# Loads of small vectors kept in program order, and two cache copies cut into sixteen in a later phase

## The chip, the cores and the metric

The kernel runs on one core of one Trainium2 chip. The metric is the device time of one execution in microseconds (us). TensorE (PE) multiplies, with its own weight-load sequencer (PEld); VectorE is DVE, ScalarE is ACT, GpSimd is POOL. SyncE (SP) computes nothing here: it issues every DMA of the kernel, one after the other.

## What is computed

One inference step of a one-layer decoder, all in float32, for a prompt group of 2048 rows and a sample group of 8 x 8 rows. The reference cut to what matters:

```
h = rms_norm(x, norm_w)
q, k, v, z_a, z_s, xbc, dt_raw, g = split(h @ w_in)
o_a = sliding-window attention(rope(norm(q)), rope(norm(k)), v, sinks)
xbc = silu(causal_conv(xbc, conv_w) + conv_b)
dt  = softplus(dt_raw + dt_bias);  A = -exp(A_log)
y   = chunked scan(x, dt, A, B, C) + D_skip * x
o_s = group_norm(y * silu(z_s)) * ssd_norm_w
out = x + (sigmoid(g_a) * (o_a * silu(z_a)) @ w_attn + sigmoid(g_s) * o_s @ w_ssd) @ w_out
k_win_sample = concat(cache_k, k_new)[:, -128:]        (the same for v)
```

The last line concerns the change: of each of the 8 samples, 120 of the 128 old rows of both caches go unchanged into an output, from DRAM to DRAM (8 x 120 x 1 KB = 960 KB for each cache).

## The kernel before

The work is in three phases. **T1** (`phase_t1`) takes the prompt in four blocks of 512 rows (b = 0 to 3): it normalizes and transposes the rows (`prep_first`, `prep_h`), stores the result to the scratch `h_d`, projects q, k, v and the attention's gate z_a, and does the attention. It begins with block 0; `prep_h` of the next block is done beside a block. **S** (`phase_s`) loads the same rows again (`load_h`), projects x, B, C, z_s and dt, and does the scan, in four blocks of four groups g (16 steps); at the end of each step `stats` sends a row of sums through DRAM (`ss_d` -> `sr` -> `rs_d`). **T2** does the samples (`phase_sa`, `phase_ss`) and the output projections.

Every float32 product is made of three matmuls: a weight tile lands in `raw` (L157, two buffers), ACT casts it into the high half of `whl` (L150), DVE makes the low half (L151), and PE multiplies (z_a: L171; q, k, v, dt: L195; phase S: L184). One load of `raw` is 1 MB, two of half that for z_a.

The program is written in one order and put into another by a scheduler, which simulates the engines and hoists work to where it thinks that it fits; an instruction under `keep_in_program_order` isn't hoisted. Each engine then runs its own list strictly in order, SP too. On SP each DMA takes the next of eight semaphores, so a DMA can't be issued before the one eight places ahead of it has completed.

The places that the change and the prediction speak of:

- `init3` (L227 to L246) loads what only phases S and T2 use: three strips of rows (conv weights, bias, norm weight), which PE transposes (L233, L234); `sinkS` in 16 loads of 8 x 1 elements (L238), which DVE negates (L239); `A_bc` (L240), which ACT exponentiates (L241) and DVE negates (L242); `dtb_bc` (L243); and `Dcol` in two loads (L246), each of 64 partitions x 16 elements of 4 bytes, taken with a stride of two from D_skip. It is called at the start of block 3 (L586), but the scheduler has put 20 of its 23 loads among those of block 0.
- L643 copies the caches; it is written in `phase_sa`, after phase S, and the scheduler has put it at the kernel's start as well.
- In T1 the first z_a tiles of block 0 end in ACT's tanh (`th`, L420) and DVE's `zs` (L421). `norm_x` of block 1 begins with ACT's square (`junk`, L251), which reads `xt`, loaded at L290. On ACT's list the first of these squares stands ahead of the third tanh.

Of the kernel before, what the change touches and what calls it, by code (L numbers as in the profile page):

```python
# [17 lines left out]
P = 128  # L18
# [60 lines left out]
def build(tc, nc, a, o, seq, phases=("T1", "S", "T2"), dbg=None):  # L79
    NB = seq // TB  # L80
    V, A, G, PE, SY = nc.vector, nc.scalar, nc.gpsimd, nc.tensor, nc.sync
# [9 lines left out]
    def ct_(name, shape, dtype=F32):  # L91
        return const.tile(shape, dtype, name=name, tag=name)
# [44 lines left out]
    sinkS = ct_("sinkS", [P, 1])  # L137
    nsinkS = ct_("nsinkS", [P, 1])
    A_bc = ct_("A_bc", [P, 32])
    dtb_bc = ct_("dtb_bc", [P, 32])  # L140
    Dcol = ct_("Dcol", [P, 16])
# [69 lines left out]
    def rpow(dst, src, scale, eps, tmp):  # L211
        G.tensor_scalar(tmp, src, scale, eps, ALU.mult, ALU.add)
        G.tensor_tensor(dst, tmp, mhalf[: dst.shape[0], : dst.shape[1]], ALU.pow)


    def init2():
# [7 lines left out]
            SY.dma_start(wrow[:, i, 72:80], w[0:8].partition_broadcast(P))  # L224
        V.tensor_scalar(wrow[:, 0], wrow[:, 0], 0.125, None, ALU.mult)

    def init3(xp, trp):  # L227
        rows = xp.tile([P, 2, P], F32, name="rows3", tag="xt")
        SY.dma_start(rows[:96, 0], a["conv_w"][0].rearrange("k (c p) -> (k c) p", p=P))
        SY.dma_start(rows[96:120, 0], a["conv_b"][0].rearrange("(c p) -> c p", p=P))  # L230
        SY.dma_start(rows[:16, 1], a["ssd_norm_w"][0].rearrange("(c p) -> c p", p=P))
        ips = trp.tile([P, 256], F32, name="tr", tag="tr")
        PE.transpose(ips[:, :120], rows[:120, 0], ident[:120, :120])  # L233
        PE.transpose(ips[:, 128:144], rows[:16, 1], ident[:16, :16])  # L234
        V.tensor_scalar(cwb.rearrange("p k c -> p (k c)"), ips[:, :120], 0.5, None, ALU.mult)
        V.tensor_copy(snw, ips[:, 128:144])
        for h in range(NH):
            SY.dma_start(sinkS[8 * h : 8 * h + 8], a["sinks"][0][h : h + 1].partition_broadcast(8))  # L238
        V.tensor_scalar(nsinkS, sinkS, -1.0, None, ALU.mult)  # L239
        SY.dma_start(A_bc, a["A_log"][0].partition_broadcast(P))  # L240
        A.activation(A_bc, A_bc, AF.Exp)  # L241
        V.tensor_scalar(A_bc, A_bc, -1.0, None, ALU.mult)  # L242
        SY.dma_start(dtb_bc, a["dt_bias"][0].partition_broadcast(P))  # L243
        dv = a["D_skip"][0].rearrange("(c l) -> l c", l=2)
        for hl in range(2):
            SY.dma_start(Dcol[64 * hl : 64 * hl + 64], dv[hl].partition_broadcast(64))  # L246

    def norm_x(xt, jp, nwb, n=P):
        st = jp.tile([P, 3], F32, name="rs", tag="rs", bufs=2)[:n]
# [61 lines left out]
    def load_h(b, smp):  # L311
        hT = []
        for k in range(KT):
            ht = cur["h"].tile([P, 2, cur["hw"]], F32R, name="hT", tag="hT")
            SY.dma_start(ht[:, :, :TB].bitcast(F32), h_d[b][k // 4][:, k % 4])
            if smp:
                split(ht[:, 0, TB:], ht[:, 1, TB:], hs[:, k])
            hT.append(ht)
        return hT
# [56 lines left out]
    def phase_t1():  # L376
        with ExitStack() as es:
# [205 lines left out]
            for b in range(NB):  # L583
                hT = nxt
                if b == NB - 1:
                    init3(xp, trp)  # L586
                for pair in range(2):
                    zs = zap.tile([P, HG, TB], F32, name="zs", tag="zs")
                    if pair == 0:
                        for hgp in range(2):  # L590
                            za_tile(b, pair, hgp, hT, zs)
                        tab = tables(b)
                        k_tile(b, hT, tab)
                        v_tile(b, hT)
                    qTs = [q_tile(b, 2 * pair + kvl, hT, tab) for kvl in range(2)]
                    if pair == 0 and b + 1 < NB:
                        prep_h(b + 1, xp, jp, trp, nwb)
                        if b + 1 == sb:
                            prep_s(xp, jp, trp, nwb)
                    if pair == 1:  # L600
                        for hgp in range(2):
                            za_tile(b, pair, hgp, hT, zs)
                    if pair == 1 and b + 1 < NB:
                        nxt = load_h(b + 1, False)
                    for tt in range(NT):
                        attn_unit(b, pair, tt, [qTs[0][tt], qTs[1][tt]], zs)

    def phase_sa(oas):
        with ExitStack() as es:
# [18 lines left out]
            for jj in range(2):  # L628
# [3 lines left out]
                for i in range(4):  # L632
                    j, hl = (4 * jj + i) // 2, (4 * jj + i) % 2
# [6 lines left out]
                SY.dma_start(kn_d[:, half * P : half * P + P], kr[64 * half : 64 * half + 64, :2].rearrange("p h d -> p (h d)"))  # L640
            for nm, scr in (("k", kn_d), ("v", vn_d)):
                ow = o[f"{nm}_win_s"]
                SY.dma_start(ow[:, 0:120], a[f"cache_{nm}"][0].rearrange("b j h d -> b j (h d)")[:, 8:P])  # L643
                SY.dma_start(ow[:, 120:P], scr.rearrange("(b t) c -> b t c", b=8))
            KN = one.tile([64, NKV, 64], F32, name="KN")
            tr = trp.tile([64, 2, P], F32, name="tr", tag="tr")
# [7 lines left out]
            for b in range(8):  # L654
# [30 lines left out]
                for pair in range(2):  # L685
                    for kvl in range(2):
                        kv = 2 * pair + kvl
                        dst = po[64 * kvl : 64 * kvl + 64, pair, b]
# [29 lines left out]
    def phase_s():  # L718
        with ExitStack() as es:
# [50 lines left out]
            def dt_block(b):  # L770
                sh = [NT, 32]
                dt = dp.tile([P] + sh, F32, name="dt", tag="dt")
                SY.dma_start(dt, dt_d[b])
                softplus(dt, dt, dtb_bc.unsqueeze(1).to_broadcast([P] + sh), P, sh, dp, "sp")
                dA = dp.tile([P] + sh, F32, name="dA", tag="dA", bufs=1)
                V.tensor_tensor(dA, dt, A_bc.unsqueeze(1).to_broadcast([P] + sh), ALU.mult)
                dA2 = dA.rearrange("p c h -> p (c h)")
                ps = trp.tile([P, 3, P], F32, name="tr", tag="tr")
                PE.matmul(ps[:, 0], tri, dA2, start=True, stop=True)
                PE.matmul(ps[:, 1], ones, dA2, start=True, stop=True)  # L780
                PE.matmul(ps[:, 2], dA2, tri, start=True, stop=True)
                acs = dp.tile([P, P], F32, name="acs", tag="acs")
                V.tensor_copy(acs, ps[:, 0])
                at = dp.tile([P, P], F32, name="at", tag="at", bufs=1)
                V.tensor_copy(at, ps[:, 2])
                SY.dma_start(ac_d[b], at)
                dec = dp.tile([P, P], F32, name="dec", tag="dec")
                A.activation(dec, ps[:, 1], AF.Exp)
                wd = dp.tile([P, P], F32, name="wd", tag="wd")
                V.tensor_tensor(wd, ps[:, 1], acs, ALU.subtract)  # L790
                A.activation(wd, wd, AF.Exp)
                V.tensor_tensor(wd, wd, dt.rearrange("p c h -> p (c h)"), ALU.mult)
                return dt.rearrange("p c h -> p (c h)"), acs, dec, wd
# [118 lines left out]
            def stats(b, g):  # L912
                r = dp.tile([P, 4], F32, name="sr", tag="sr")
                SY.dma_start(r, ss_d[b][g].rearrange("o (p c) -> p (o c)", c=4))
                r2 = dp.tile([P, 4], F32, name="sr2", tag="sr2")
                rpow(r, r, 1.0 / 512, 4 * EPS, r2)
                SY.dma_start(rs_d[b][g].rearrange("(p c) -> p c", c=4), r)

            for b in range(NB):
                dts_ = dt_block(b)  # L920
                hT = load_h(b, b == sb)
                for g in range(4):
                    ssd_group(b, g, *proj_group(b, g, hT), *dts_)
                    stats(b, g)
            cur["hT"] = hT
            for g in range(4):
                tr = trp.tile([P, 4, P], F32, name="tr", tag="tr")
# [358 lines left out]
    if "S" in phases:  # L1286
        phase_s()
# [41 lines left out]
```

## Time and profile before

| | |
|---|---|
| median of 3 runs | 3202.14 us (3200.97 to 3202.41) |
| the profiled execution's own time | 3201.39 us |
| its span | 3199.6 us |
| PE / DVE / ACT / POOL busy | 96% / 65% / 44% / 31% |
| mean granted TensorE clock | 0.989 of full speed |

The profile comes from one execution. The span is the time from the first to the last instruction that the profiler saw; 1.8 us of the execution lie outside it. Times in the views are counted from the span's start. Block 3 of T1 begins at about 620 us, phase S at about 717, T2 at about 2000.

### The profile page before, as it was taken

How to read it: one execution, taken by the hardware profiler on the slowest of the kernel's cores; microseconds unless marked ns; L12 is line 12 of the kernel's file. 1: busy time of each engine (PE TensorE's matmuls, PEld its weight loads, DVE VectorE, ACT ScalarE, POOL GpSimd, SP SyncE). 2: the span in 40 equal slices, each digit the busy share in tenths (PEclk: the TensorE clock that was granted, in tenths of full speed). 3: DMA queues.
4: the chain of work that ended last, by engine and by line, in shares of the span. 5: the costliest groups of instructions: out<-in, count | busy, mean ns of one | idle time of the engine just before them, and what ended most of it. 6: DMA issues, size and time to landing. Idle time of an engine off the chain costs nothing.

```text
span 3199.6 us, 49248 instructions
## 1 busy us (share of the span) xinstructions
PE 3085.4 (96%) x19038; PEld 2649.2 (83%) x19038; DVE 2081.5 (65%) x3265; ACT 1419.9 (44%) x2786; POOL 982.5 (31%) x905
## 2 busy tenths in 40 slices
PE   6999999998999999999999998999999999999999
PEld 5978787877899877777777776787877799999888
DVE  3877868787777787888878886455555554334433
ACT  3544535455555555555656564333233333222321
POOL 1523232231445555555656664000121100000000
PEclk8999999999999999999999998999999999999999
DMA  6544425333433544444454444445655564345443
GB/s 215 157 141 117 141 76 180 108 107 103 126 121 119 172 130 124 154 148 131 129 167 147 129 141 128 139 131 154 205 181 143 155 206 132 99 132 175 137 107 103
DMA packets 472931, 448.88 MB, mean 140 GB/s; under 512 B 33824, under 2 KB 420664, under 8 KB 472648
## 3 DMA queue, kind: packets, MB, share of 16 engines
q1 hardware_dynamic: 472696, 445.73, 45.2%
q8 instruction: 150, 2.46, 0.3%
q14 instruction: 85, 0.70, 0.1%
HBM read 382.39 MB, written 65.35 MB: 140 GB/s over the span
## 4 chain that ended last, share of the span: by engine, by line
PE 73%; DVE 12%; DMA 5%; POOL 5%; issue 3%; ACT 2%; SPq 0%; POOLq 0%; DVEq 0%; ACTq 0%
PE mm L184 46%; PE mm L195 12%; PE mm L171 5%; DVE acc L760 3%; DVE whl L151 2%; POOL L L857 2%; DMA raw<-in_w_in_dram 2%; PE sc L522 1%; PE tr L551 1%; POOL ws L881 1%; DVE zs L897 1%; PE tr L539 1%; PE st L884 1%; DMA xt<-in_x_prompt_dram 1%; ACT whl L150 1%
## 5 line engine op out<-in xcount | busy, mean ns | idle before, releaser
L184 PE MATMUL mm<-hT,whl 128*128 128x512 f32 (+1 forms) x6720 | 1349.1, 357 | 10.4 <-DMA hT<-h_d 4.1
L184 PEld LDWEIGHTS mm<-hT,whl 128*128 128x128 f32 x6720 | 1119.5, 190 | 181.1 <-issue 12.6
L151 DVE TENSOR_TENSOR whl<-raw,whl 128x2048 fp32r<-128x2048 f32 (+1 forms) x232 | 524.6, 2265 | 280.4 <-ACT whl L150 273.0
L184 PE MATMUL mm<-ot,whl 128*128 128x512 f32 (+1 forms) x2880 | 569.1, 355 | 2.8 <-DVE whl L151 2.5
L184 PEld LDWEIGHTS mm<-ot,whl 128*128 128x128 f32 x2880 | 474.2, 188 | 74.9 <-issue 5.7
L150 ACT CAST whl<-raw 128x2048 fp32r<-128x2048 f32 (+1 forms) x232 | 412.7, 1786 | 263.3 <-PE mm L184 132.5
L195 PE MATMUL mm<-whl,hT 128*128 128x256 f32 (+1 forms) x2304 | 307.8, 289 | 23.7 <-DVE zs L421 17.2
L195 PEld LDWEIGHTS mm<-whl,hT 128*128 128x128 f32 x2304 | 290.7, 192 | 28.2 <-DVE zs L421 17.9
L760 DVE SCALAR_TENSOR_TENSOR acc<-cr,cwb,acc 128x512 f32<-128x512 f32 x288 | 284.5, 990 | 15.8 <-ACT acc L755 7.0
L857 POOL TENSOR_TENSOR L<-L,cbm 128x1024 f32<-128x1024 f32 x64 | 182.5, 2861 | 94.4 <-DVE cbm L846 92.8
L195 PE MATMUL mm<-whl,ot 128*128 128x256 f32 (+1 forms) x1632 | 203.9, 285 | 0.0
L195 PEld LDWEIGHTS mm<-whl,ot 128*128 128x128 f32 (+1 forms) x1632 | 197.6, 188 | 5.3 <-issue 4.9
L171 PE MATMUL mm<-hT,whl 128*128 128x512 f32 x768 | 194.3, 403 | 2.3 <-ACT hT L277 2.1
L855 ACT ACTIVATE L<-AB,acs 128x128 f32<-128x128 f32 x512 | 157.0, 389 | 38.6 <-PE py L878 29.0
L171 PEld LDWEIGHTS mm<-hT,whl 128*128 128x128 f32 x768 | 142.8, 192 | 33.8 <-ACT hT L277 2.5
L368 ACT ACTIVATE s<-s,ng 128x128 f32<-128x128 f32 x256 | 99.9, 393 | 94.4 <-DVE ng L362 84.2
L150 ACT CAST ot<-v 128x512 fp32r<-128x512 f32 x96 | 58.9, 620 | 162.1 <-DVE v L1195 86.9
L881 POOL TENSOR_TENSOR ws<-wx,ws 128x512 fp32r<-128x512 f32 x64 | 112.2, 1752 | 10.1 <-ACT ws L880 9.8
L374 POOL TENSOR_SCALAR s<-s,den 128x128 f32<-128x128 f32 x128 | 50.1, 403 | 202.7 <-DVE den L370 140.6
L826 ACT ACTIVATE th<-mm 128x512 f32<-128x512 f32 (+1 forms) x80 | 40.0, 509 | 160.8 <-PE mm L184 153.6
L764 ACT ACTIVATE th<-acc 128x512 f32<-128x512 f32 x96 | 60.5, 630 | 111.8 <-DVE acc L760 111.7
L1187 ACT ACTIVATE t<-mm 128x512 f32<-128x512 f32 (+1 forms) x76 | 37.6, 518 | 162.4 <-PE mm L184 141.9
(318 smaller groups left out, 3912.5 us busy)
## 6 DMA issues: line engine op xcount, KB each, us to landing
raw<-in_w_in_dram SPq DMA_DIRECT2D x120, 1024.0 KB
hT<-h_d SPq DMA_DIRECT2D x80, 512.0 KB
raw<-in_w_in_dram SPq DMA_DIRECT2D x64, 512.0 KB
AB<-ac_d SPq DMA_DIRECT2D x64, 512.0 KB
raw<-in_w_ssd_proj_dram SPq DMA_DIRECT2D x32, 1024.0 KB
v_d<-zs SPq DMA_DIRECT2D x16, 1024.0 KB
v<-v_d SPq DMA_DIRECT2D x64, 256.0 KB
raw<-in_w_attn_proj_dram SPq DMA_DIRECT2D x64, 256.0 KB
```

Source lines behind the costliest of these rows:

```text
L150: A.copy(hi, src)
L151: V.tensor_tensor(lo, src, hi.bitcast(F32), ALU.subtract)
L171: PE.matmul(ps, hl[:, x, k, c0 : c0 + P], ht[:, y, :], start=first and i == 0, stop=last and i == n - 1,)
L184: PE.matmul(ps, hl[:, x, k, c0 : c0 + P], ht[:, y, lo : lo + n], start=i == 0, stop=i == 3 * len(hT) - 1,)
L195: PE.matmul(ps, ht[:, x, tt * P : tt * P + m], hl[:, y, k, :n], start=i == 0, stop=i == 3 * len(hT) - 1,)
L368: A.activation(s[:, i, :width], s[:, i, :width], AF.Exp, bias=ng[:, i : i + 1], accum_out=den[:, i : i + 1])
L374: G.tensor_scalar(s[:, i, :width], s[:, i, :width], den[:, i : i + 1], 0.5, ALU.mult, ALU.mult)
L760: V.scalar_tensor_tensor(out=acc, in0=raw[:, k : k + TB], scalar=cwb[:, k, ct : ct + 1], in1=acc, op0=ALU.mult, op1=ALU.add)
L764: A.activation(th, acc, AF.Tanh)
L855: A.activation(L[:, h], AB[:, h], AF.Relu, scale=-1.0, bias=acs[:, hc.start + h : hc.start + h + 1])
L857: G.tensor_tensor(L, L, cbm[:, c].unsqueeze(1).to_broadcast([P, 8, P]), ALU.mult)
L881: G.tensor_tensor(ws[:, 1], wx, ws[:, 0].bitcast(F32), ALU.subtract)
```

## The change

A helper `late` issues a DMA that is kept in program order. All 23 loads of `init3` go through it. The two cache copies leave `phase_sa`; in their place phase S copies one sample's rows of k and one sample's of v (120 KB each, 16 x 1920 elements) behind `stats` of groups 1 and 3 of each block, 16 DMAs in all, through `late` as well.

```diff
+    def late(dst, src):
+        tc.keep_in_program_order(SY.dma_start(dst, src))
+
     def init3(xp, trp):
         rows = xp.tile([P, 2, P], F32, name="rows3", tag="xt")
-        SY.dma_start(rows[:96, 0], a["conv_w"][0].rearrange("k (c p) -> (k c) p", p=P))
+        late(rows[:96, 0], a["conv_w"][0].rearrange("k (c p) -> (k c) p", p=P))
...
         for h in range(NH):
-            SY.dma_start(sinkS[8 * h : 8 * h + 8], a["sinks"][0][h : h + 1].partition_broadcast(8))
+            late(sinkS[8 * h : 8 * h + 8], a["sinks"][0][h : h + 1].partition_broadcast(8))
         V.tensor_scalar(nsinkS, sinkS, -1.0, None, ALU.mult)
-        SY.dma_start(A_bc, a["A_log"][0].partition_broadcast(P))
+        late(A_bc, a["A_log"][0].partition_broadcast(P))
...
-            SY.dma_start(Dcol[64 * hl : 64 * hl + 64], dv[hl].partition_broadcast(64))
+            late(Dcol[64 * hl : 64 * hl + 64], dv[hl].partition_broadcast(64))
...
                 ow = o[f"{nm}_win_s"]
-                SY.dma_start(ow[:, 0:120], a[f"cache_{nm}"][0].rearrange("b j h d -> b j (h d)")[:, 8:P])
                 SY.dma_start(ow[:, 120:P], scr.rearrange("(b t) c -> b t c", b=8))
...
                     stats(b, g)
+                    for nm in ("k", "v"):
+                        for r in range((4 * b + g) * 8 // (4 * NB), (4 * b + g + 1) * 8 // (4 * NB)):
+                            late(o[f"{nm}_win_s"][r, 0:120], a[f"cache_{nm}"][0, r, 8:P].rearrange("j h d -> j (h d)"))
```

What this does to the engines' lists stands below at three places. With the change, line numbers are three higher from L227 on, two higher behind L643 (L157 and the others ahead of `init3` stay); the loads and copies that go through `late` bear its line, L228.

**The start, SP.** Before, from the last of the small loads on (`xt` is block 1's input, `h_d` a store of the normalized rows, `raw` a weight tile):

```order
L240 DMA A_bc<-in_A_log_dram 128x32
L282 DMA h_d_1_61<-hT 128x1024
L243 DMA dtb_bc<-in_dt_bias_dram 128x32
L246 DMA Dcol<-in_D_skip_dram 64x16x1 x2
L290 DMA xt<-in_x_prompt_dram 128x1024
L282 DMA h_d_1_61<-hT 128x1024
L290 DMA xt<-in_x_prompt_dram 128x1024
L643 DMA out_dram<-in_cache_k_dram 8x2x15360
L282 DMA h_d_1_61<-hT 128x1024
L643 DMA out_dram<-in_cache_v_dram 8x2x15360
L157 DMA raw<-in_w_in_dram 128x8x256 x3
```

The same stretch of SP's list with the change:

```order
L577 DMA tab_2442<-in_rope_p_dram 128x4x80
L285 DMA h_d_1_61<-hT 128x1024 x2
L293 DMA xt<-in_x_prompt_dram 128x1024 x2
L285 DMA h_d_1_61<-hT 128x1024 x2
L157 DMA raw<-in_w_in_dram 128x8x256 x3
L476 DMA dt_d_112<-dtt 128x128
```

The 20 small loads and both copies are gone from this stretch; both loads of `xt` stand behind two stores of `h_d` and nothing of `init3`. ACT's list loses the exponential of A_bc, DVE's the negations of sinkS and A_bc; the rest keeps its order.

**T1's last block, SP and PE.** SP before, at the start of block 3 (`oa_d` is a store of block 2's attention, `dt_d` of its dt; the six `raw` of 128x8x128 are the next z_a tiles):

```order
L157 DMA raw<-in_w_in_dram 128x8x256
L563 DMA oa_d_1_73<-zs 128x4x128
L473 DMA dt_d_115<-dtt 128x128
L157 DMA raw<-in_w_in_dram 128x8x128 x6
L157 DMA raw<-in_w_in_dram 128x8x256
```

With the change:

```order
L157 DMA raw<-in_w_in_dram 128x8x256
L566 DMA oa_d_1_73<-zs 128x4x128
L228 DMA rows_6540<-in_conv_w_dram 96x128
L228 DMA rows_6540<-in_conv_b_dram 24x128
L228 DMA rows_6540<-in_ssd_norm_w_dram 16x128
L228 DMA sinkS<-in_sinks_dram 8x1 x16
L228 DMA A_bc<-in_A_log_dram 128x32
L228 DMA dtb_bc<-in_dt_bias_dram 128x32
L228 DMA Dcol<-in_D_skip_dram 64x16x1 x2
L476 DMA dt_d_115<-dtt 128x128
L157 DMA raw<-in_w_in_dram 128x8x128 x6
```

All 23 loads now stand ahead of the six z_a loads. PE's list there before, around the transposes of the strips (`tr<-PT,vT` is an attention output, `tr<-cst,kd` transposes k):

```order
L551 MATMUL tr<-PT,vT 64x512 x4
L233 MATMUL tr<-cst,rows_6540 128x120
L234 MATMUL tr<-cst,rows_6540 128x16
L453 MATMUL tr<-cst,kd 128x128 x4
L195 MATMUL mm<-whl,hT 128x256 x38
```

PE's list at the same place with the change:

```order
L554 MATMUL tr<-PT,vT 64x512 x4
L195 MATMUL mm<-whl,hT 128x256 x80
L236 MATMUL tr<-cst,rows_6540 128x120
L237 MATMUL tr<-cst,rows_6540 128x16
L456 MATMUL tr<-cst,kd 128x128 x4
L195 MATMUL mm<-whl,hT 128x256 x38
```

80 matmuls have come ahead of the two transposes. On DVE's list the copies out of the transposes, the negation of sinkS and that of A_bc stand a little behind them, on ACT's the exponential of A_bc behind the cast of the next weight tile.

**The end of T1, PE.** Before, from the last products of T1 (L171) to the first of phase S (L184); `tr<-cst,s` and `tr<-PT,vT` belong to the attention, `tr<-cst,qr` transposes the last q:

```order
L171 MATMUL mm<-hT,whl 128x512 x12
L539 MATMUL tr<-cst,s 128x128 x4
L551 MATMUL tr<-PT,vT 64x512 x4
L496 MATMUL tr<-cst,qr 128x128 x12
L184 MATMUL mm<-hT,whl 128x288 x20
L522 MATMUL sc<-KTT,qT 128x256 x4
```

With the change:

```order
L171 MATMUL mm<-hT,whl 128x512 x6
L542 MATMUL tr<-cst,s 128x128 x8
L554 MATMUL tr<-PT,vT 64x512 x4
L499 MATMUL tr<-cst,qr 128x128 x8
L525 MATMUL sc<-KTT,qT 128x256 x4
L499 MATMUL tr<-cst,qr 128x128 x4
L184 MATMUL mm<-hT,whl 128x288 x23
```

One attention unit more stands between the last products of T1 and the first of phase S. In phase S itself the lists of PE, DVE, ACT and POOL keep their order; SP's gets the copies, each pair right behind the store `rs_d` of its step.

## Rows read from the trace of the kernel before

**Rows 1.** The page: busy us (share of the span) xinstructions.

```profile
PE 3085.4 (96%) x19038; PEld 2649.2 (83%) x19038; DVE 2081.5 (65%) x3265; ACT 1419.9 (44%) x2786; POOL 982.5 (31%) x905
```

**Rows 2.** Waits, 40 to 84 us: total us, times, longest.

```profile
DVE zs L421 <- ACT th L420: 22.0, 2, 21.3
ACT junk L251 <- DMA xt<-in_x_prompt_dram: 21.9, 2, 20.9
PE mm L195 <- DVE zs L421: 17.2, 2, 16.1
...
DVE nsinkS L239 <- DMA h_d<-hT: 5.1, 1, 5.1
ACT A_bc L241 <- DMA A_bc<-in_A_log_dram: 5.0, 1, 5.0
...
PE mm L195 <- DVE dtt L472: 1.5, 1, 1.5
```

**Rows 3.** Timeline of PE, 40 to 84 us: start, duration, what, [idle before].

```profile
44.29 5.96 PE L195 MATMUL mm<-whl,hT 128*128 128x256 f32 x48 [1.12 <-DVE zs L421]
66.34 14.12 PE L195 MATMUL mm<-whl,hT 128*128 128x256 f32 x89 [16.10 <-DVE zs L421]
```

**Rows 4.** Timeline of SP, 40 to 70 us.

```profile
40.59 1.44 SPq L246 DMA_DIRECT2D Dcol<-in_D_skip_dram  x2
42.13 3.15 SPq L290 DMA_DIRECT2D xt<-in_x_prompt_dram  x1
...
58.14 0.80 SPq L643 DMA_DIRECT2D out_dram<-in_cache_k_dram  x1
```

**Rows 5.** DMA, 43 to 61 us, in 40 slices of 0.45 us.

```profile
GB/s 6 6 0 0 0 0 0 0 0 0 0 0 0 0 0 0 0 0 0 0 0 0 0 0 0 0 0 0 0 0 0 0 0 0 0 0 0 0 0 110
DMA packets 1957, 0.06 MB, mean 3 GB/s; under 512 B 1945, under 2 KB 1945, under 8 KB 1957
```

**Rows 6.** Two windows: us, busy of five engines, PEclk, DMA share, GB/s.

```profile
64.00:73.00 9.00, 6.66 (x33) 6.66 (x34) 6.71 (x7) 5.79 (x9) 1.46 (x4) 0.53 0.92 374
66.40:75.10 8.70, 8.70 (x51) 8.70 (x51) 6.10 (x6) 4.29 (x7) 2.47 (x4) 0.65 0.76 295
```

**Rows 7.** Groups of PE by form, 66.3 to 75.1 us: xcount | busy, mean ns | idle before.

```profile
L195 PE MATMUL mm<-whl,hT 128*128 128x256 f32 x48 | 8.7, 362 | 16.1 <-DVE zs L421 16.1
```

**Rows 8.** Timeline of SP, 575 to 735 us.

```profile
621.01 0.39 SPq L157 DMA_DIRECT2D raw<-in_w_in_dram  x1
...
622.13 0.50 SPq L473 DMA_DIRECT2D dt_d<-dtt  x1
636.63 43.27 SPq L157 DMA_DIRECT2D raw<-in_w_in_dram  x7
```

**Rows 9.** Windows of block 3, columns as in rows 6.

```profile
575.00:690.00 115.00, 115.00 (x852) 103.53 (x852) 88.27 (x194) 54.12 (x159) 44.63 (x56) 1.00 0.28 80
636.60:642.40 5.80, 5.80 (x51) 5.80 (x50) 4.59 (x10) 1.76 (x3) 3.11 (x3) 1.00 0.69 184
```

**Rows 10.** Timeline of PE, 600 to 760 us, then 673 to 676, and of ACT, 615 to 682.

```profile
619.45 0.32 PE L233 MATMUL tr<-cst,rows 120*128 120x120 f32 x1
...
620.28 4.75 PE L195 MATMUL mm<-whl,hT 128*128 128x256 f32 x38
...
673.17 2.25 PE L171 MATMUL mm<-hT,whl 128*128 128x512 f32 x9
...
659.32 1.99 ACT L150 CAST whl<-raw 128x1024 fp32r<-128x1024 f32 x2
```

**Rows 11.** Waits of PE, 690 to 770 us.

```profile
PE tr L551 <- DVE PT L541: 5.2, 5, 2.0
PE tr L496 <- DVE qr L351: 4.7, 1, 4.7
```

**Rows 12.** Phase S: a window, and waits of PE from 780 to 2000 us.

```profile
800.00:1950.00 1150.00, 1114.40 (x6554) 942.42 (x6552) 901.01 (x1059) 660.98 (x1188) 648.34 (x505) 1.00 0.43 137
...
PE mm L184 <- DMA hT<-h_d: 4.1, 2, 2.7
```

More of the change, by code (lines that the diff above doesn't have):

```diff
@@ L225, in init2 @@
         V.tensor_scalar(wrow[:, 0], wrow[:, 0], 0.125, None, ALU.mult)
+    def late(dst, src):
+        tc.keep_in_program_order(SY.dma_start(dst, src))
     def init3(xp, trp):
         rows = xp.tile([P, 2, P], F32, name="rows3", tag="xt")
-        SY.dma_start(rows[:96, 0], a["conv_w"][0].rearrange("k (c p) -> (k c) p", p=P))
-        SY.dma_start(rows[96:120, 0], a["conv_b"][0].rearrange("(c p) -> c p", p=P))
-        SY.dma_start(rows[:16, 1], a["ssd_norm_w"][0].rearrange("(c p) -> c p", p=P))
+        late(rows[:96, 0], a["conv_w"][0].rearrange("k (c p) -> (k c) p", p=P))
+        late(rows[96:120, 0], a["conv_b"][0].rearrange("(c p) -> c p", p=P))
+        late(rows[:16, 1], a["ssd_norm_w"][0].rearrange("(c p) -> c p", p=P))
         ips = trp.tile([P, 256], F32, name="tr", tag="tr")
@@ L237, in init3 @@
         for h in range(NH):
-            SY.dma_start(sinkS[8 * h : 8 * h + 8], a["sinks"][0][h : h + 1].partition_broadcast(8))
+            late(sinkS[8 * h : 8 * h + 8], a["sinks"][0][h : h + 1].partition_broadcast(8))
         V.tensor_scalar(nsinkS, sinkS, -1.0, None, ALU.mult)
-        SY.dma_start(A_bc, a["A_log"][0].partition_broadcast(P))
+        late(A_bc, a["A_log"][0].partition_broadcast(P))
         A.activation(A_bc, A_bc, AF.Exp)
         V.tensor_scalar(A_bc, A_bc, -1.0, None, ALU.mult)
-        SY.dma_start(dtb_bc, a["dt_bias"][0].partition_broadcast(P))
+        late(dtb_bc, a["dt_bias"][0].partition_broadcast(P))
         dv = a["D_skip"][0].rearrange("(c l) -> l c", l=2)
         for hl in range(2):
-            SY.dma_start(Dcol[64 * hl : 64 * hl + 64], dv[hl].partition_broadcast(64))
+            late(Dcol[64 * hl : 64 * hl + 64], dv[hl].partition_broadcast(64))
     def norm_x(xt, jp, nwb, n=P):
```

## The prediction

> **What bounds the kernel now.** I read first the page's busy times: PE computes 96% of the span, 3085.4 of 3199.6 us [rows 1]. So PE's list is the kernel, and a change can win or lose only in the 114 us in which PE stands still or in stretches at a lower clock. The list of waits, taken where the moved loads stand, shows the largest single idle stretch of the program: PE waits 16.1 us for one `zs` of DVE, which waits for ACT's tanh, which stands on ACT's list behind the square of the next block's `xt`, which waits 20.9 us for the load of `xt` [rows 2]. PE ran 48 matmuls from 44.29 to 50.25 and the next began at 66.34 [rows 3].
>
> Why `xt` is late is to be seen in two more views. SP issued the two `Dcol` loads at 40.59, and `xt` right behind them at 42.13 [rows 4]. From 44 us to 60.5 the DMA engines move nothing that counts: 1945 packets under 512 bytes, 0 GB/s, then 110 in the last slice [rows 5]. `Dcol` is 2 x 64 x 16 = 2048 elements of 4 bytes taken with a stride, and 1945 packets is nearly all of them. So each element goes as a packet of its own, 1945 in the 17.5 us of those slices, 111 a microsecond: 2048 / 111 = 18.5 us in which everything issued later queues. Not the number of loads but this one pair holds the queue.
>
> **The start.** With the change the loads of `xt` have neither `Dcol` nor the other small loads ahead of them, and no copies behind them before the next weight tiles. Real transfers in this stretch run at 295 to 374 GB/s [rows 6], so 512 KB of `xt` take 1.4 to 1.8 us. Issued at 42.1 at the latest, `xt` should land by 46, against 63.9 now. Square, tanh and `zs` behind it take about 2.5 us; the third `zs` is due at 50.25 and should be done by 49. What goes, term by term:
> - 16.1 us, the wait itself [rows 2]. If `xt` were still a little late, some of it stays; I keep 13 as the lower end.
> - 1.1 us ahead of the 48 matmuls [rows 3]: there DVE had waited 5.1 us to negate sinkS and ACT 5.0 for A_bc [rows 2]. Both instructions leave.
> - 1.5 us for `dtt` [rows 2]: its weight tile was queued behind both copies, which with `xt` fill the rings for most of 64 to 73 [rows 6].
> - 2.7 us of clock: after the stall the same 48 matmuls take 8.7 us instead of 5.96 [rows 3, 7], and the granted clock over that stretch is 0.65 [rows 6], a mixture of the lower level and the full one. Without the idle time ahead of it, the clock should stay at the full level.
>
> Sum: -16.1 - 1.1 - 1.5 - 2.7 = **-21.4 us** (ends -16 and -22; a little more could come from weights that land earlier).
>
> **T1's last block.** The 23 loads now stand there, ahead of six z_a loads. PE has no gap from 575 to 690 [rows 9], so a gain is excluded and a loss is not. Three waits are added.
> - The z_a weights. SP idles there from 622.6 to 636.63 [rows 8], and this idle time is what hides the loads. By the eight semaphores, the fourth sinkS load waits until the weight tile issued at 621.01 has landed; 1 MB takes 5.8 us here [rows 9], so until some 627.5. Sixteen further small loads at 0.35 us put `Dcol` at about 633.5. Its 18.5 us of packets then end at about 653, the first z_a pair (1 MB, 5.8 us) lands at about 659, and its cast on ACT ran at 659.32 [rows 10]. It is a close thing: a delay of 0 to 3 us of ACT. PE first uses that tile at 673.17 [rows 10], so the delay reaches PE only through what stands behind the cast on ACT.
> - PE's two transposes. They now come 80 matmuls later; 38 take 4.75 us [rows 10], so 80 take 10.0 and PE reaches them at 619.45 + 10.0 = 629.5. The strips are issued right behind the weights and land a little after 627.5. Cost 0 to 1; PE's whole list is queued behind them.
> - DVE's negations and ACT's exponential wait for loads issued by 633: 0 to 3 us each, on engines with idle time there.
>
> Bounds: 0, and the whole block as at the start, 18.5 + 2.7 for the clock = 21. I take **+2**, near the lower end, because the idle time of SP and rings (DMA share 0.28 [rows 9]) covers nearly all of it.
>
> **The end of T1.** PE loses 5.2 us there to attention masks and 4.7 to a last q [rows 11]. With the new list one more attention unit falls between T1's last products and phase S's first, and its softmax stands behind weight splits on ACT and DVE. Bounds: -4.7 (that wait goes) and +10 (one more of the same size as both). I take **+2**, since PE has one more unit of chained work there and fewer independent products beside it.
>
> **Phase S.** The copies move the same bytes as before. Sixteen issues at 0.8 us [rows 4] are 13 us of SP. In the rings the two whole copies and the `xt` beside them had 9.0 us [rows 6], so a sixteenth takes some 0.56. In phase S the DMA engines are busy 0.43 of the time, and in the whole phase PE waited for a DMA twice, 4.1 us together, both times for `hT` [rows 12]. Those loads follow the `rs_d` of group 2; the copies follow groups 1 and 3, so they don't meet. Bounds: 0, and all exposed, 16 x (0.8 + 0.56) = 22. I take **+0.5**, as two waits in 1220 us are near to none.
> The Trainium skill speaks against this part: "DMA: Bandwidth & Descriptors", Anatomy of one DMA, gives each DMA a fixed cost of about 2.0 us (fitted there on the GpSimd path). For 14 DMAs more that is 28 us, an estimate from that page, and by it the forecast below would be 3213. No run here shows that price on SP's queue.
>
> **The sum.** -21.4 + 2 + 2 + 0.5 = -16.9 on the profiled execution's 3201.39 gives 3184.5. The median of the runs lies 0.75 us above that execution, so I write 3185.2 us.
>
> **The rivals.**
> 1. `Dcol`'s block of 18.5 us only moves. If PE stands still for all of it in block 3 and finds the lower clock afterwards, 21 of the 21.4 come back: 3202.14 - 21.4 + 21 + 2.5 = 3204, no change that counts. For it: the z_a tile comes out within a microsecond of its cast. Against it: 14 us between that cast and PE's first use.
> 2. The end of T1 becomes dearer, by 10 instead of 2: 3193. For it: PE already idles there and the clock falls with it; the chained unit has little beside it.
> 3. `xt` stays late, because stores of `h_d` and weight tiles still fill the queue ahead of it. Then only the small waits go, some -5 and +4.5: 3202, no change. Against it: the empty rings behind 44 us [rows 5].
> 4. The other side: each copy in phase S holds what SP has behind it. In order behind `rs_d`, a pair delays the next weight or `AB` load by 2 x (0.8 + 0.56) = 2.7 us at each of 8 places, 22 in all; if PE stands still each time and half the clock cost of the start (1.35) follows, 11 more. That gives 3202.14 - 16.9 - 0.5 + 33 = 3218. It decides from 23 us on, where 3208.5 is passed, so only if most of the 8 places stall. Against it: in that phase PE waited for a DMA twice, never at such a place [rows 12].
> The rule of the Trainium skill named under phase S points to this rival, and the rows so far do not bear it out.
>
> **How the numbers follow.** The forecast has 0.72, rival 2 0.14, rival 1 0.08, rival 3 0.03, rival 4 0.03. A measurement of this kernel can tell 0.2%, 6.4 us, from no change: faster means below 3195.7, slower above 3208.5. Forecast and rival 2 are faster: 0.86; rivals 1 and 3 the same: 0.11; rival 4 slower: 0.03. The range: upwards it takes in rival 2 and a part of block 3's bound, to 3196; downwards the end of T1 at -4.7 instead of +2, to 3178.
>
> **What would show it.** Right: no DMA-empty stretch at 44 to 60 us, PE's first idle stretch over 5 us gone, full clock from 50 on; a stretch of tiny packets at about 634 to 653 instead, with PE at most 3 us idle in block 3; no new wait of PE for a DMA in phase S. Wrong: a PE gap of 10 us or more between 629 and 690 (less the gain), or `hT` and `raw` among PE's releasers at the copies' places.

## The result and the profile after

The change made the kernel faster: 3181.36 us in the median of 4 runs (3180.89 to 3185.55) against 3202.27 of the kernel before (3200.97 to 3208.05), a ratio of 0.9934 with a 95% interval of 0.9917 to 0.9951. The forecast was 3185.2, within 3178 to 3196. The profiled execution has a span of 3179.3 us, 20.3 less than before [rows 1]. The page after: busy us, share, instructions.

```profile
PE 3080.3 (97%) x19038; PEld 2643.1 (83%) x19038; DVE 2081.8 (65%) x3265; ACT 1421.5 (45%) x2786; POOL 983.1 (31%) x905
```

**The start.** The timeline of PE, 38 to 80 us, answers to [rows 3]: no gap between the two stretches of 256-wide matmuls, and the first transposes of k at 58.91, where they had been at 80.30.

```profile
42.17 16.91 PE L195 MATMUL mm<-whl,hT 128*128 128x256 f32 x136
58.91 0.60 PE L456 MATMUL tr<-cst,kd 128*128 128x128 f32 x4
...
64.02 0.60 PE L456 MATMUL tr<-cst,kd 128*128 128x128 f32 x4
```

The second transposes of k, at 64.02, stood at 87.18 in the kernel before, behind its wait for `dtt` (timeline of PE before, 43 to 150 us):

```profile
80.30 0.60 PE L453 MATMUL tr<-cst,kd 128*128 128x128 f32 x4
...
83.35 3.99 PE L195 MATMUL mm<-whl,hT 128*128 128x288 f32 x28 [1.52 <-DVE dtt L472]
...
87.18 0.60 PE L453 MATMUL tr<-cst,kd 128*128 128x128 f32 x4
```

ACT still waits for `xt`, but briefly (waits, 38 to 84 us, to be held against [rows 2]):

```profile
ACT junk L254 <- DMA xt<-in_x_prompt_dram: 4.3, 1, 4.3
```

The timeline of SP, 16 to 44 us, has its issue at 30.12, twelve microseconds earlier than in [rows 4]:

```profile
30.12 1.30 SPq L293 DMA_DIRECT2D xt<-in_x_prompt_dram  x2
```

**T1's last block.** The timeline of SP, 585 to 735 us, has the moved loads:

```profile
600.65 9.01 SPq L228 DMA_DIRECT2D sinkS<-in_sinks_dram  x16
...
610.59 1.40 SPq L228 DMA_DIRECT2D Dcol<-in_D_skip_dram  x2
```

The DMA view of 600 to 660 us, in 40 slices of 1.5 us, shows the pair's stretch of next to no bytes there, from about 612 to 630 us:

```profile
GB/s 297 338 167 8 0 0 0 8 10 4 0 0 0 0 0 0 0 0 0 0 91 282 267 243 288 252 47 0 173 330 196 11 0 0 0 0 0 38 322 337
```

The cast of the z_a weights that queued behind it came at 637.79, which is the 659.32 of [rows 10] less 21.5, so it was hardly later than the gain allows (ACT's timeline, 592 to 655 us):

```profile
637.79 1.99 ACT L150 CAST whl<-raw 128x1024 fp32r<-128x1024 f32 x2
```

One wait of PE ends between 560 and 690 us; it is the only row of its waits there:

```profile
PE mm L195 <- issue: 2.2, 1, 2.2
```

**The end of T1.** Here time is lost. Timelines of PE, ACT and DVE, 670 to 705 us: PE waits 8.3 us for the scaling `s` of a softmax. On ACT its exponentials (L371) stand behind two weight casts of phase S, 3.7 us, and on DVE the scaling stands behind their splits, 4.5 us.

```profile
695.03 1.13 PE L542 MATMUL tr<-cst,s 128*128 128x128 f32 x4 [8.30 <-DVE s L375]
...
687.16 3.70 ACT L150 CAST whl<-raw 128x2048 fp32r<-128x2048 f32 x2
690.76 0.24 ACT L150 CAST hT<-hs 128x64 fp32r<-128x64 f32 x1
690.91 0.40 ACT L371 ACTIVATE s<-s,ng 128x128 f32<-128x128 f32 x1
...
689.10 4.49 DVE L151 TENSOR_TENSOR whl<-raw,whl 128x2048 fp32r<-128x2048 f32 x2 [0.16 <-ACT whl L150]
...
694.60 0.61 DVE L375 TENSOR_SCALAR s<-s,den 128x128 f32<-128x128 f32 x2
```

**Phase S.** PE waits for `hT` as it did before [rows 12], and for no other DMA (waits of PE, 780 to 2000 us).

```profile
PE mm L184 <- DMA hT<-h_d: 4.1, 2, 2.4
```

**Where along the program the time was won.** The table takes five matmuls that every version has, and gives how much earlier (minus) PE started them than in the kernel before, from the timelines of PE (the last column: where PE's last matmul ends). Rows E are the experiments below. Two profiles of one and the same kernel are the first two rows; they tell how far single numbers can be trusted. In E1 and E2 8 and 24 more matmuls stand ahead of the first transposes of k than in the change (144 and 160 against 136), so their first column is too small by the time of these.

| | first transposes of k, 80.30 | z_a in block 3, 673.17 | first xT in phase S, 805.26 | first product of T2, 2012.29 | PE's end, 3196.42 |
|---|---|---|---|---|---|
| the change | -21.4 | -22.4 | -15.6 | -17.3 | -20.4 |
| the change again (E12) | -20.1 | -19.7 | -12.5 | -11.8 | -14.8 |
| E1 Dcol's pair alone moved | -11.0 | -16.8 | -16.2 | -16.7 | -13.4 |
| E2 loads alone | -14.9 | -23.6 | -16.7 | -17.8 | -18.4 |
| E3 copies alone | -1.2 | -1.7 | -1.1 | -1.8 | -3.6 |
| E4 all hoisted, D_skip as a row | -17.1 | -15.3 | -15.7 | -15.8 | -14.8 |
| E5 init3 in block 1 | -21.3 | -4.8 | -7.8 | -9.5 | -9.6 |
| E7 Dcol twice | -22.2 | -5.2 | +1.1 | +1.7 | +0.4 |
| E8 change, D_skip as a row | -21.1 | -26.1 | -17.8 | -13.4 | -16.3 |
| E9 change, strips hoisted | -20.1 | -19.9 | -19.4 | -19.9 | -17.2 |
| E10 E9, D_skip as a row | -20.0 | -19.3 | -18.9 | -18.0 | -15.2 |
| E11 only sinkS late, D_skip as a row | -20.2 | -22.5 | -21.8 | -18.7 | -16.6 |

E6 has no row, because its list puts the first xT ahead of work that stands before it elsewhere. It has -20.4 at z_a, -10.5 at the second step's first xT (where the change has -15.6, E12 -11.3, E9 -18.1 and E10 -17.7), -10.0 at T2's first product and -3.2 at PE's end.

### The profile page after: what moved, and what is told of

Read it like the earlier page. It is cut to its first block, busy times and chain, and to the rows that moved or that the text cites. A ratio compares the mean times of both kernels' runs of the same rounds, so it can differ in the third digit from the quotient of the medians.

```text
span 3179.3 us, 49256 instructions
## 1 busy us (share of the span) xinstructions
PE 3080.3 (97%) x19038; PEld 2643.1 (83%) x19038; DVE 2081.8 (65%) x3265; ACT 1421.5 (45%) x2786; POOL 983.1 (31%) x905
## 4 chain that ended last, share of the span: by engine, by line
PE 76%; DVE 12%; POOL 5%; DMA 3%; issue 3%; ACT 1%; SPq 0%; POOLq 0%; DVEq 0%; ACTq 0%
PE mm L184 47%; PE mm L195 13%; PE mm L171 5%; DVE acc L762 3%; POOL L L859 2%; DVE whl L151 2%; PE tr L554 2%; PE sc L525 1%; POOL ws L883 1%; DVE zs L899 1%; PE tr L542 1%; DMA hT<-h_d 1%; PE st L886 1%; DMA raw<-in_w_in_dram 1%; POOL hd L892 1%
## 5 line engine op out<-in xcount | busy, mean ns | idle before, releaser
L184 PE MATMUL mm<-hT,whl 128*128 128x512 f32 (+1 forms) x6720 | 1345.4, 356 | 10.1 <-DMA hT<-h_d 4.1
L184 PEld LDWEIGHTS mm<-hT,whl 128*128 128x128 f32 x6720 | 1116.0, 189 | 180.9 <-issue 14.2
L184 PE MATMUL mm<-ot,whl 128*128 128x512 f32 (+1 forms) x2880 | 568.1, 354 | 0.0
L184 PEld LDWEIGHTS mm<-ot,whl 128*128 128x128 f32 x2880 | 474.1, 188 | 71.2 <-issue 5.7
L762 DVE SCALAR_TENSOR_TENSOR acc<-cr,cwb,acc 128x512 f32<-128x512 f32 x288 | 284.9, 992 | 15.6 <-ACT acc L757 7.0
L171 PE MATMUL mm<-hT,whl 128*128 128x512 f32 x768 | 192.7, 401 | 2.3 <-ACT hT L280 2.3
L171 PEld LDWEIGHTS mm<-hT,whl 128*128 128x128 f32 x768 | 142.4, 191 | 32.5 <-ACT hT L280 2.7
L371 ACT ACTIVATE s<-s,ng 128x128 f32<-128x128 f32 x256 | 99.8, 392 | 87.5 <-DVE ng L365 80.3
```

What stands on the lines that cost most here:

```text
L171: PE.matmul(ps, hl[:, x, k, c0 : c0 + P], ht[:, y, :], start=first and i == 0, stop=last and i == n - 1,)
L184: PE.matmul(ps, hl[:, x, k, c0 : c0 + P], ht[:, y, lo : lo + n], start=i == 0, stop=i == 3 * len(hT) - 1,)
L371: A.activation(s[:, i, :width], s[:, i, :width], AF.Exp, bias=ng[:, i : i + 1], accum_out=den[:, i : i + 1])
L762: V.scalar_tensor_tensor(out=acc, in0=raw[:, k : k + TB], scalar=cwb[:, k, ct : ct + 1], in1=acc, op0=ALU.mult, op1=ALU.add)
```

## The experiments

The theory: the single-element packets of Dcol's pair held the queue at the start; in block 3 their some 18 us are covered; the loss at T1's end is one of order. Against it stood that the number of small loads, the place of the copies, or the late loads in block 3 explain the same rows. Each ratio is taken against the kernel before as run beside the experiment, where its median lay between 3204.75 and 3206.34 us; so ratios are to be compared, not times.

**E1: the pair alone.** All else as before.

```diff
     def init3(xp, trp):
+        dv = a["D_skip"][0].rearrange("(c l) -> l c", l=2)
+        for hl in range(2):
+            late(Dcol[64 * hl : 64 * hl + 64], dv[hl].partition_broadcast(64))
         rows = xp.tile([P, 2, P], F32, name="rows3", tag="xt")
```

> Only the two Dcol loads are moved, to the start of T1's last block; the 21 other small loads and both whole cache copies stay hoisted to the kernel's start, where the copies now stand directly ahead of xt. Theory A (the pair's single-element packets hold the queue): the stretch with empty DMA engines at 44 to 60 us is gone; PE's wait of 16.1 us for zs falls to about 5 us, what is left being the 9 us of both copies ahead of xt; PE's order at the end of T1 is that of before, so nothing is lost there; about 3190 us. Rival B (it is the number of small loads and their waits that holds xt): 21 of 23 loads are still there, the wait stays at 14 us or more, 3200 us or above.

Measured: 3184.58 us, ratio 0.9936 (0.9921 to 0.9951). With 18 small loads left at the start (the strips had always been later), the wait of 16.1 us is gone; 3.7 us of another wait took its place (waits of PE, 36 to 86 us):

```profile
PE mm L195 <- DVE qn L337: 3.7, 1, 3.7
PE mm L195 <- DVE zs L424: 1.2, 1, 1.2
```

The pair is the cause; rival B falls as to the large part. The ratio is that of the whole change (0.9934): two moved loads of 23, and no copy, gain as much, as T1's end then loses little (-16.8 and -16.2).

**E2 and E3: each half of the change alone.** E2 has the late loads and the copies of before; E3 has the copies in phase S and the loads of before.

> All 23 small loads late as in the change, but the two cache copies whole and hoisted as before; T1's end has the changed order on PE. Theory A: the start wins about 20 us (the copies, now early in the queue, may give back 1 to 3 of it), T1's end loses 6 to 7 as in the change; about 3188 us. Rival C (the copies' place makes the gain at the start): the stall of 16 us stays and the time is 3205 or more, since T1's end still loses.

> Only the copies are moved, in 16 parts in phase S; init3 as before, hoisted. Theory A: the wait of 16.1 us for zs stays, the 1.5 us behind it goes; phase S neither wins nor loses more than 1 us; what T2's start wins in the change (some 5 us) shows here if it comes from the copies' place in SP's list: 3195 to 3200 us. Rival C: the stall goes with the copies, 3183 or less. Rival D (each part of the copies costs about 2 us): 3225.

Measured: E2 3189.99 us, ratio 0.9949 (0.9933 to 0.9966); E3 3202.16 us, ratio 0.9991 (0.9982 to 1.0001). E3 keeps a wait of 15.96 us for `zs`, and phase S passes without loss: the copies neither made the gain nor cost anything that can be measured; rivals C and D fall. In E2 the scheduler put both whole copies ahead of the weight tile that SP issues third. At the first transposes of k E2 stands 6.5 us behind the change (-14.9 and -21.4), in part because 24 more matmuls stand ahead of them; by block 3 nothing is left of it (-23.6 and -22.4). T1's end loses 6.9 us in E2, as in the change.

**E4: nothing moved but the copies, and the packets taken away.**

```diff
-        for hl in range(2):
-            SY.dma_start(Dcol[64 * hl : 64 * hl + 64], dv[hl].partition_broadcast(64))
+        SY.dma_start(Drow, a["D_skip"][0].partition_broadcast(P))
+        dv = Drow.rearrange("p (c l) -> p l c", l=2)
+        for hl in range(2):
+            V.tensor_copy(Dcol[64 * hl : 64 * hl + 64], dv[64 * hl : 64 * hl + 64, hl])
```

> Copies in phase S as in the change, all small loads hoisted to the start as before, but D_skip is loaded as one contiguous row of 32 to every partition (128 packets of 128 bytes instead of 2048 of 4) and DVE takes the two strided halves from it. Theory A: the empty stretch of the DMA engines and the wait of 16.1 us are gone though every load stands where it stood; the small waits of the start (about 1 us) stay, T1's end keeps the order of before: start -19 to -21, about 3177 to 3181 us, as good as the change or better. Rival B (number and place of the loads): 3197 to 3200.

Measured: 3186.2 us, ratio 0.9943 (0.9928 to 0.9958). In the timeline of PE, 36 to 86 us, the third stretch begins at 50.99 behind a wait of half a microsecond:

```profile
44.47 5.98 PE L196 MATMUL mm<-whl,hT 128*128 128x256 f32 x48 [1.02 <-DVE zs L426]
50.99 6.10 PE L196 MATMUL mm<-whl,hT 128*128 128x256 f32 x49 [0.54 <-DVE zs L426]
```

So a load of D_skip at the same place holds PE for half a microsecond at most once its last dimension is contiguous. The start, -17.1, is 3.0 and 4.3 us short of the change's in its two profiles, and short of my -19 to -21; E11 is about that.

**E5: the block laid elsewhere.** The change with `if b == 1:` for the call of init3.

> The change, but init3 is called at the start of T1's block 1 instead of block 3. PE's and ACT's lists at the end of T1 differ from the change: the last softmax stands ahead of phase S's first two weight casts. Theory A (the change loses 6.4 us at T1's end through that order alone): start -23 us as in the change; Dcol's 18.7 us of packets hide in block 1 as in block 3, at most 3 us; T1's end loses 0 to 2 us; about 3175 us. Rival E (the loss at T1's end has to do with the late loads in block 3 or is made by any order without the early stall): still 8 us of idle PE there, 3181.

Measured: 3192.92 us, ratio 0.9969 (0.9956 to 0.9982): the gain halves. T1's end loses nothing with this order (-4.8 at z_a, -7.8 behind it), as theory A had it, but of the 21.3 us won at the start 16.5 are lost by block 3. The place is in block 1 (waits, 255 to 300 us):

```profile
DVE qr L354 <- POOL qr L349: 18.7, 1, 18.7
...
ACT junk L254 <- DMA xt<-in_x_prompt_dram: 17.2, 2, 16.6
...
PE tr L499 <- DVE qr L354: 14.2, 1, 14.2
```

It is the stall of the start again: the chain goes from `xt` over ACT's square and POOL's `qr` to DVE's and to PE. In blocks 0 to 2 `norm_x` of the next block stands in ACT's list and waits for `xt` behind the packets; block 3 is the only one that prepares no next block. I had forecast "at most 3 us" and missed that.

**E6: T1's end by itself.** On the change, the first casts and splits of phase S (the first two calls of `split`) are kept in program order.

> The change, with the casts and splits of phase S's first weight tiles kept in program order, so that on ACT and DVE the softmax of T1's last attention unit stands ahead of them; PE's list at T1's end is that of the change but for four matmuls. Theory A: PE's wait of 8.3 us for the softmax's scaling falls to 3 to 4.5 us, T1's end loses 1 to 3 us instead of 6.4; about 3177 us. Rival E (the time only moves): PE waits as long behind it for the split weights, 3181.

Measured: 3194.23 us, ratio 0.9965 (0.9951 to 0.998), slower than the change. PE's waits, 670 to 770 us:

```profile
PE mm L188 <- ACT whl L150: 6.8, 1, 6.8
PE tr L546 <- DVE s L379: 6.6, 3, 3.7
```

The wait of 8.3 fell to 3.7 as theory A said, but the second kept cast then stood too late and PE waited 6.8 us for it: rival E's way. From z_a to the second step's xT E6 loses 9.9 us, the change 6.8. The run shows the cause of the 8.3 us and is no cure. Another 6.8 us went in T2, where four windows of 30 us from 2050 on, with PE busy throughout, show a granted clock of 0.92 to 0.97.

**E7: how much cover block 3 had left.** On the change, a second pair of the same loads into an unused tile.

> The change, with Dcol loaded twice at its place in block 3 (the second time into a tile that nobody reads): 4096 single-element packets, some 37 us of queue. Theory A (block 3 hides one block because PE first uses the z_a weights 9.5 us after they are split): the second 18.7 us are hidden by those 9.5 and cost 9 to 13 us with the clock; about 3192 us. Rival F (hidden altogether): 3181. Rival G (nothing was left over): 3200 or more.

Measured: 3200.41 us, ratio 0.9987 (0.9978 to 0.9997). Waits, 630 to 700 us:

```profile
ACT whl L151 <- DMA raw<-in_w_in_dram: 18.7, 1, 18.7
...
PE sc L527 <- DVE s L534: 16.1, 1, 16.1
```

Rival G: nothing was left over. ACT waits for the weights as long as the second block is, with the attention's copies and exponentials behind it in order; on DVE the mask's copies of the scores `s` stand behind the split of these weights. PE waits for those, not for the z_a weights themselves. The 9.5 us between split and first use hid nothing.

**E8: the change without the packets in block 3** (E4's edit on the change).

> The change, with D_skip loaded as one contiguous row (128 packets of 128 bytes) and split by DVE, at the same place in block 3. Theory A: the 18.7 us of single-element packets vanish from block 3; PE gains nothing by it but perhaps the 2.2 us that it waited there; T1's end keeps the order and the loss of the change: 3178 to 3181 us. If 5 us or more are gained, the block was not hidden in the change.

Measured: 3184.22 us, ratio 0.9938 (0.9923 to 0.9953). PE's wait of 2.2 us in block 3 is gone, and no other time; T1's end has its 8.3 us. From the transposes of k in block 1 (-24.3) to z_a (-26.1) E8 gains 1.9 us, the change 0.2. So in the change the block was hidden but for some 2 us.

**E9 and E10: T1's end without the reordering.** E9 is the change with the strips and their transposes left to the scheduler (plain `SY.dma_start`, written after the late loads); E10 has the contiguous row besides.

> The change, but the three strips of rows and their two transposes are left to the scheduler as before (it puts them into block 2 again); the other 20 loads stay late. PE's list at T1's end is then word for word that of before, with Dcol's pair still in block 3. Theory A (the loss of 6 to 7 us at T1's end comes from the order that the strips' transposes push along): start -23 us, block 3 the same as in the change, T1's end loses 0 to 1 us, so 5 to 7 us below the change. Rival E (T1's end loses because the late loads delay its engines): 8 us of idle PE there, the same as the change within 2 us.

> The former with D_skip loaded as one contiguous row: no single-element packets anywhere. Theory A: as the former, or up to 3 us better where the block of 18.7 us had cost something in block 3; 5 to 9 us below the change.

Measured, on one chip with E11 and E12: E9 3184.2 us, ratio 0.9929 (0.9916 to 0.9942); E10 3186.84 us, ratio 0.9944 (0.9931 to 0.9957). PE's list at T1's end is that of before, and so are its waits in E9 (670 to 770 us), to be held against [rows 11]:

```profile
PE tr L554 <- DVE PT L544: 5.2, 5, 2.0
PE tr L499 <- DVE qr L354: 4.7, 1, 4.7
```

From z_a in block 3 to the first xT of phase S, E9 loses 0.5 us and E10 0.4 where the change loses 6.8 and 7.2; up to the second step's xT it is 1.8 and 1.6 against 6.8 and 8.4. So three loads and two transposes of 0.3 us, moved by 10 us in a list, led the scheduler to an order at T1's end that costs some 5 to 7 us. T2 then gave more than half of it back: E9 is 8.1 us ahead of E12 at T2's first product and 2.4 at PE's end. The medians differ from E12's by 4.6 us for E9 and 1.9 for E10, less than the 5 to 7 and 5 to 9 that I had forecast, within intervals that overlap.

**E11 and E12: the small loads' own part, and a control.** E11 keeps only the 16 sinkS loads late; E12 is the change itself.

> Copies in phase S, D_skip as one contiguous row hoisted to the start with A_log, dt_bias and the strips, and only the 16 sinkS loads late. The run with every small load hoisted and one row won 17.8 us at the start where the change won 23.1. Theory A (what was missing, 5 us, is the 16 small loads on SP ahead of the weights): start -22 to -23 here. Rival H (it is DVE's and ACT's waits for A_bc, dt_bias and D_skip): start -18 to -19.

> The change itself, on the chip of the three others, so that they are compared with it directly: about 0.993 of the kernel before, with 8.3 us of idle PE at T1's end.

Measured: E11 3184.45 us, ratio 0.9929 (0.9915 to 0.9943); E12 3188.77 us, ratio 0.9946 (0.9932 to 0.996). The start of E11 (-20.2) equals that of E12 (-20.1); with the sinkS loads hoisted, E4 had -17.1 there and -17.0 at the transposes of k in block 1, where E11 has -22.3. So 16 loads of 32 bytes cost 3 to 5 us at the start, as they stand on SP ahead of weights and `xt`; rival H falls. The figure rests on one profile of each, and the two profiles of the change differ by 1.3 and 2.3 us at these two places.

No version beats the change by more than the measurement tells; E9 and E11 have the lowest ratio.

## Why the prediction was right

- **The start, -21.4.** Right in cause, and within 2 us in size. The pair's packets are the cause (E1, E4). The Trainium skill, "DMA: Bandwidth & Descriptors", Rules for kernel authors, says that a strided or non-contiguous last dimension becomes one descriptor per element. The 1945 packets of [rows 5] agree, and with a contiguous row PE's wait fell from 16.1 to 0.5 us (E4). That the first transposes of k came 21.4 us earlier, as in the sum, is chance, for the wait for `dtt`, one of its terms, stands behind them. At the second transposes the change is 23.2 us ahead and E12 21.8. Term by term, from the timelines of PE: 2.1 us ahead of the 48 matmuls (E12 0.8) against my 1.1; the wait of 16.1 in full; 3.2 for the slow matmuls behind the stall against 2.7; 1.8 between the first and second transposes against 1.5.
- **T1's last block, +2.** The size was right (2.2 us of idle PE, 1.4 in E12, gone in E8), by luck: none of my three waits reached PE (the last section has what is known of the 2.2). The margin was not what I said either. "14 us between that cast and PE's first use" was my argument against rival 1, and E7 refutes it: PE waits for the softmax, which stands behind the cast on ACT and behind the split on DVE. The block ended just in time: a second one cost 17 us at z_a (-22.4 and -5.2). Rival 1 had the right mechanism and missed by its cover alone.
- **The end of T1, +2.** The mechanism was named, the size was wrong: 6.8 and 7.2 us between z_a and phase S (6.8 and 8.4 up to its second step), within the bounds of -4.7 to +10. I took one more unit of chained work as 2; what counts is that a softmax stands behind two casts and two splits, 3.7 and 4.5 us, which is read from the lists and the durations of each.
- **Phase S, +0.5.** Right: the waits for `hT` are the same 4.1 us, and E3 shows no loss. The Trainium skill, "DMA: Bandwidth & Descriptors", Anatomy of one DMA, gives each DMA a fixed cost of about 2.0 us, fitted on the GpSimd path; for 14 DMAs more that was an estimate of 28 us. E3, which has them, shows no such loss (ratio 0.9991).
- **What I had no term for.** T2's start, whose order the change also shifts, won some 3 us in both profiles of the change (-17.3 to -20.4, -11.8 to -14.8). In the waits of the kernel before (PE, 1995 to 2200 us) stands one that the change does not have:

```profile
PE mm L184 <- DVE whl L151: 2.5, 1, 2.5
```

  A wait like it, of 2.1 to 2.9 us, stands in E1 to E4, E6 and E9 to E11. It is gone in the change, E12, E5, E7 and E8, so only where both the strips are late and the copies are in phase S (E6 has both and keeps it). From T2's first product to PE's end these five win 0.1 to 3.1 us; the others range from a gain of 1.8 (E3) to a loss of 6.8 (E6). That the missing wait is the 3 us is therefore not shown; falls of the clock (last section) move T2 as well.
- **The total.** That PE's end came out 3.5 us from the forecast's -16.9 is in part luck. By the table the start and block 3 won 3.0 us more than their terms, phase S 2.2 and T2 3.1; T1's end lost 4.8 more.

## What to carry to other kernels

A small DMA is judged by its packets, not by its bytes: two loads of 4 KB held the queue for some 18 us, and with one contiguous load and two 0.17 us copies on chip PE's wait fell from 16.1 to 0.5 us. Find the load that matters and move that one: the pair alone (E1) gained what all 23 loads and both copies did. Before such a load is moved, look at which in-order engine will wait behind it at the new place (a load that feeds the next block's first step, a cast with a softmax behind it), not at when its own result is first used. Where a scheduler orders the program, compare the lists far from the edit as well: here a third of the gain was lost 100 us after the moved loads, through order alone.

## What the runs showed of the hardware

- PE's granted clock falls for short whiles also in stretches that the profile counts as fully busy. In E9 the windows read 0.94 and 1.00 of full speed, 0.06 of 30 us being 1.8 us; three windows of T2 like the first stand in E9, two in the change.

```profile
2062.00:2092.00 30.00, 30.00 (x172) 24.18 (x172) 16.66 (x29) 8.41 (x13) 0.00 (x0) 0.94 0.43 124
2152.00:2182.00 30.00, 30.00 (x165) 24.26 (x165) 11.84 (x28) 8.27 (x16) 0.00 (x0) 1.00 0.33 83
```

  Cut finer, such a window shows the lower of the two levels, 1.2 of 2.4 GHz, behind a row of short matmuls of the samples' attention, 128x32, 64x128 and 64x8 where the products around them are 128x512 (E9: windows, then the timeline of PE, 2078 to 2096 us):

```profile
2083.00:2087.00 4.00, 4.00 (x41) 3.08 (x40) 2.11 (x4) 0.00 (x0) 0.00 (x0) 1.00 0.04 9
2087.00:2090.00 3.00, 3.00 (x9) 2.32 (x8) 0.83 (x5) 1.19 (x4) 0.00 (x0) 0.52 0.60 170
...
2085.74 0.30 PE L692 MATMUL po<-PTn,vn 8*64 8x32 f32 x2
2085.96 0.44 PE L672 MATMUL sc<-KC,QS 64*32 64x128 f32 x8
2086.21 0.24 PE L673 MATMUL sc<-KN,QS 64*32 64x8 f32 x8
```

  All eight falls between 2010 and 2200 us, in the profiles of the kernel before, the change, E9 and E12, begin within a microsecond of the end of such a row; most rows pass without one. Time goes with the clock: of the eleven runs of the kernel before beside E9 the fastest, 3199.99 us, has a mean granted clock of 0.990 and the slowest, 3212.59, one of 0.986. So the falls are likely part of the spread between executions of one kernel, and of the differences in the table's last column.

- In block 3 of the change PE stood still for 2.2 us with no semaphore outstanding ("issue" among the releasers). The same stands in E2, E6, E7, E9 and E12 (1.3 to 2.0 us), which have Dcol's packets there behind 18 or more small loads; it is absent from E8, E10 and E11, which have none, and from E1. In each of these six profiles a transfer of the instruction queue (q8 in the DMA view, in slices of 2 us) lies in the last four microseconds before PE goes on, the first for 26 to 30 us. That PE's instructions arrived late is therefore likely, but not shown.
